# A hybrid decoder layer on one core: four experts of a block side by side, expert weights in 8 KB runs, spread products four in a row

## The chip, the core and the metric

The kernel runs on one NeuronCore of one Trainium2 chip. TensorE (PE) multiplies, VectorE (DVE), ScalarE (ACT) and GpSimd (POOL) do elementwise work, and SyncE (SP) issues nearly all loads; its own queue is called SPq in the profile. The metric is the device time of one execution in microseconds. Before the change the median of three runs is 867.6 us (866.16 to 868.55).

## The reference

One layer over 256 tokens of width 1024, all in float32. The first half (norm, input projection, a causal convolution, differential attention, output projection) is left by the change as it is. The second half is a mixture of experts:

```
h2 = rms_norm(x, norm2_g) * (1 + sc2) + sh2
scores = sigmoid(t @ w_router);  choice = scores + router_bias
# 4 of 8 groups, then 8 of 64 experts per token; gates = normed scores * 2.5
g, u = split(einsum('td,edf->tef', t, w_gu), 2)          # w_gu:   64 x 1024 x 512
routed = einsum('tef,efd->td', silu(g) * u * gate, w_down)   # w_down: 64 x 256 x 1024
x = x + g2 * (routed + shared_expert(t))
```

sc2, sh2 and g2 are slices of the conditioning product `silu(c) @ w_ada + b_ada`. All 64 experts are loaded once: 2 MiB of gate/up weights and 1 MiB of down weights each, 192 MiB in all.

## The kernel before

The kernel writes its instructions itself, in an order that a small planner in the same file sets when the program is built. Pieces of work are generators; each yields what it needs (an engine and an estimated cost, a buffer, an event), and the planner always issues the piece that can start first, by priority among near ties. What comes out is one fixed program for each engine, and each engine runs its own in order. The planner's cost of a matrix step is 0.87 whether it holds one, two or four products.

**Experts.** The routing (about 310 to 340 us) sorts the experts by the number of their tokens and puts them into 28 blocks of 128 rows ("slots"). A block is one of four kinds: H (one expert of 128 rows), M (two, with 96 and 32 rows; the 96 are multiplied as three 32-column tiles), P (two of 64) and Q (four of 32). The order is three P blocks, then PAT, `QPQQPQPPPMPHPMMMHPMPMPQPP` (line 35). I count blocks from 0: the early Q blocks are 3, 5, 6 and 8, and the late one is 25.

A block goes through these steps:
- `gather` (line 1507): a comparison on DVE makes a selection matrix, PE multiplies the split tokens with it (line 1532), for two blocks at once, and ACT applies scale and shift (line 1499) into `xt`.
- `experts` (line 1771): the gate/up product, line 1785. For each of K = 8 slices of the 1024 features, one product per tile; tiles of one block write to different rows of one bank, so they use different columns of the array. In a Q block, `parts` (line 338) cuts the four experts into two pairs, and the eight slices run first for one pair, then for the other.
- `gate_up` (line 1600): silu on ACT, product with the gate on DVE, two transpositions on PE (line 1613), a copy on ACT (line 1617).
- `tail` (line 1656): the down product, line 1676, for f in 2 slices and h in 2 halves of the output, again pair by pair in a Q block. Then per half h: times g2 on DVE (line 1688), a split into two reduced-precision halves (lines 1745 and 1747), and the products that spread the block's 128 rows over the tokens (line 1699), two for each of the 2 token tiles t, each tile into a bank of its own; DVE adds the bank to x (line 1703).
- The last block is cut finer (`finale`, `spread`) to shorten its end.

**Loads.** Weights go in pieces of 1 MiB into slots of 8 KB per partition. In the expert stage 14 slots are in turn; `advance` (line 366) gives the next piece of a fixed list to a slot as soon as the planner has the slot's last reader, and `load` (line 389) issues it on SP, behind a wait for that reader. A gate/up matrix is two pieces (halves of the 1024 rows), a down matrix one. Line 409 maps row k * 128 + p to partition p, so in a gate/up piece each partition gets four rows of 2 KB that lie 256 KB apart in memory, and in a down piece two rows of 4 KB. The first pieces of w_ada (kind "b", 256 columns) have rows of 1 KB.

**Columns.** The scale and shift of the second norm (`a2c`, `b2c`), one number per feature, must lie along partitions in the same order as the features in `h2T` and `xt`: feature k * 128 + p at partition p, column k. `ada` (line 736) makes them from the conditioning product's chunks 6 to 9: a copy to SBUF, four transpositions (line 762), and small sums on DVE.

Of the kernel before, what the change touches and what calls it, by code (L numbers as in the profile page):

```python
# [199 lines left out]
def tile_hybrid_block(ctx, tc, x, c, positions, w_ada, b_ada, norm1_g, w_in, conv_dw, conv_dw_b,  # L200
# [91 lines left out]
    params += [(rbias, bcast(router_bias, NE)), (wr, w_router[0].rearrange("(k p) n -> p k n", p=P))]  # L292
# [45 lines left out]
    def parts(kd):  # L338
        ts = tiles_of[kd]
        return [ts[0:2], ts[2:4]] if kd == "Q" else [ts]  # L340

    for b, (kd, js) in enumerate(blocks):
        gs = []
        for ts in parts(kd):
            es = sorted({t[0] for t in ts})
            gs += [("g", js[e], q) for q in range(2) for e in es]
        ds = [("d", j, 0) for j in js]
        if b == len(blocks) - 1:
            ds = [("d", j, 0, cs) for cs in ENDS for j in js]
            gs = [("g", j, q, c_) for q in range(2) for c_ in range(2) for j in js]  # L350
        order += gs + ds
# [37 lines left out]
    def load(kind, i, q, cut, now):  # L389
# [19 lines left out]
        wsrc = wsrc.rearrange("(k p) n -> p k n", p=P)  # L409
# [107 lines left out]
    pcol = cst.tile([P, 96], F32, name="pcol")  # L517
    ss = cst.tile([P, 8], F32, name="ss")
# [15 lines left out]
    nc.gpsimd.dma_start(rawb[33:49], b_ada[0, 3 * D:5 * D].rearrange("(k p) -> k p", p=P))  # L534
    nc.scalar.dma_start(rawb[49:57], vec(norm2_g, P))
# [94 lines left out]
    def late_columns():  # L630
# [3 lines left out]
        nc.tensor.transpose(p[:, 0:57], rawb[0:57], ident[0:57, 0:57])  # L634
        yield AP(57)
        nc.scalar.copy(pcol[:, 32:89], p[:, 0:57])
# [92 lines left out]
    p2 = cst.tile([P, 2, K], F32, name="p2")  # L729
# [6 lines left out]
    def ada(i, pool):  # L736
# [22 lines left out]
        else:  # L759
            yield "P", 0.43  # L760
            for j in range(4):
                nc.tensor.transpose(p[:, j * P:(j + 1) * P], s[:, j * P:(j + 1) * P], ident)
            yield pl.ev("cols")
            j = 4 * (i - 6)
            o = p2.rearrange("p a k -> p (a k)")[:, j:j + 4]
            yield TS(4)
            nc.vector.tensor_reduce(o, p.rearrange("p (j g r) -> p j g r", j=4, g=4)[:, :, :, 0], axis=AX.X, op=OP.add)
            yield TS(4)
            nc.vector.tensor_tensor(o, o, pcol[:, 65 + j:69 + j], op=OP.add)
            jj = slice(j % 8, j % 8 + 4)  # L770
            yield TS(4)
            if i < 8:
                nc.vector.tensor_copy(b2c[:, jj], p2[:, 0, jj])
            else:
                nc.vector.scalar_tensor_tensor(a2c[:, jj], p2[:, 1, jj], 1.0, pcol[:, 81:89][:, jj], op0=OP.add,
                                               op1=OP.mult)
# [462 lines left out]
    def turn(t, q):  # L1239
        d = slice(q * 512, (q + 1) * 512)  # L1240
        e = yield [TS(512), AS(512)]
        if e == "A":
            nc.scalar.activation(xn2[:, t, d], x_sb[:, t, d], AF.Copy, scale=rs2[:, t, 3:4])
        else:
            nc.vector.tensor_scalar(xn2[:, t, d], x_sb[:, t, d], rs2[:, t, 3:4], None, op0=OP.mult)
# [354 lines left out]
    def gate_up(pg, gate, put=None):  # L1600
# [11 lines left out]
        for f in range(2):  # L1612
            nc.tensor.transpose(pg[:, f * P:(f + 1) * P], act[:, f * P:(f + 1) * P], ident)
# [42 lines left out]
    def tail(b, pg):  # L1656
# [10 lines left out]
        for ts in parts(kd):  # L1667
            es = sorted({t[0] for t in ts})
            for e in es:
                yield pl.ev("L", "d", js[e], 0)  # L1670
                yield max(loaded["d", js[e]].at)
            for f in range(2):
                for h in range(2):
                    yield "P", 0.87
                    for e, o, m in ts:
                        nc.tensor.matmul(pd[h][o:o + m], aT[:, f, o:o + m],  # L1676
                                         loaded["d", js[e]].k[f][:, h * 512:(h + 1) * 512],
# [263 lines left out]
```

## Time and profile before

| what | us |
|---|---|
| median of 3 runs | 867.6 (866.16 to 868.55) |
| the profiled execution | 866.95 |
| its span, first to last instruction | 865.2 |
| PE busy | 809.2 |
| DVE busy | 464.9 |
| ACT busy | 311.2 |
| bytes read | 269.11 MB, 312 GB/s over the span |

The profile is one execution. Its page gives busy times of each engine, then 40 equal slices (21.6 us each) with the busy share in tenths, the clock that TensorE was granted (PEclk), the share of the 16 DMA engines and GB/s. "PE" counts products as they were issued; a pipelined product overlaps the next, so the step from one start to the next tells more than a single duration. A float32 product shows as two records. Views by window give, for a stretch, its length, the busy time of each engine with counts, the granted clock, the DMA share and GB/s. A row of the timeline gives start, duration, engine, line, operation, tile written <- tiles read, partitions x elements, and the number of records merged.

### The profile page before, as it was taken

To read this page: it belongs to the slowest core of one execution; us is meant where nothing else is said; L and a number is where in the kernel's file an instruction comes from. 1 tells how busy PE (TensorE), PEld (TensorE's weight loads), DVE (VectorE), ACT (ScalarE), POOL (GpSimd) and SP (SyncE) were. 2 spreads that over 40 slices of the span, in tenths; PEclk is the share of its full clock that TensorE was granted. 3 is DMA by queue.
4 is the path that set the end of the run, shared out by engine and by line. 5 is a ranking of instruction groups with operands and counts; after the bars stand their busy time and mean duration, and the time that the engine had idled before them with its cause. 6 is when DMAs were issued, how large, how long until landed. Compare 5 with 4: busy or idle time off the path is not lost.

```text
span 865.2 us, 13140 instructions
## 1 busy us (share of the span) xinstructions
PE 809.2 (94%) x4731; PEld 455.6 (53%) x4731; DVE 464.9 (54%) x1083; ACT 311.2 (36%) x682; POOL 191.6 (22%) x242
## 2 busy tenths in 40 slices
PE   3999999999858999999999999999999999999997
PEld 2897766798738776535342433434344343444233
DVE  6559999999975874206242343253433534433333
ACT  4457758667656542203020321212122121232010
POOL 3004899887514740001000000000000000000000
PEclk9999999999967999999999999999999999999999
DMA  9998678558446554999999999999999999979981
GB/s 322 366 340 288 209 253 299 184 207 273 162 152 240 187 197 176 354 389 393 355 394 397 392 397 393 392 397 393 394 392 395 374 341 362 355 278 388 398 303 50
DMA packets 127339, 271.03 MB, mean 313 GB/s; under 512 B 7085, under 2 KB 16901, under 8 KB 127272
## 3 DMA queue, kind: packets, MB, share of 16 engines
q1 hardware_dynamic: 126936, 270.00, 85.2%
q8 instruction: 37, 0.61, 0.3%
q14 instruction: 30, 0.25, 0.1%
q0 software_dynamic: 272, 0.16, 0.1%
q10 hardware_dynamic: 64, 0.02, 0.0%
HBM read 269.11 MB, written 1.05 MB: 312 GB/s over the span
## 4 chain that ended last, share of the span: by engine, by line


## 5 line engine op out<-in xcount | busy, mean ns | idle before, releaser
L1785 PE MATMUL bank<-fa 128*32 128x512 f32 (+2 forms) x1048 | 228.0, 596 | 0.1
L1703 DVE TENSOR_TENSOR fa<-fa,bank 128x512 f32<-128x512 f32 x108 | 73.3, 685 | 108.7 <-PE bank L1699 108.7
L1785 PEld LDWEIGHTS bank<-fa 128*32 128x32 f32 (+2 forms) x1048 | 63.5, 122 | 123.6 <-issue 119.2
L873 DVE SCALAR_TENSOR_TENSOR bank<-fa,tap,bank 128x256 f32<-128x256 f32 x232 | 112.9, 486 | 5.6
L1676 PE MATMUL bank<-fa 128*32 128x512 f32 (+2 forms) x496 | 111.5, 602 | 4.3 <-ACT fa L1617 4.2
L1745 ACT CAST obs<-fa 128x512 fp32r<-128x512 f32 x54 | 33.3, 619 | 150.6 <-DVE fa L1688 139.3
L1699 PE MATMUL bank<-obs,ra 128*128 128x512 f32 x216 | 78.1, 450 | 1.8 <-ACT obs L1745 0.6
L786 POOL TENSOR_TENSOR rb<-fa,rb 128x512 fp32r<-128x512 f32 x44 | 58.6, 1338 | 71.1 <-ACT rb L805 66.9
L1499 ACT ACTIVATE fa<-bank,b2c,a2c 128x256 f32<-128x256 f32 x108 | 53.2, 562 | 44.2 <-PE bank L1532 44.1
L786 POOL TENSOR_TENSOR ra<-fa,ra 128x512 fp32r<-128x512 f32 x48 | 63.9, 1339 | 21.2 <-ACT ra L805 20.6
L1699 PEld LDWEIGHTS bank<-obs,ra 128*128 128x128 f32 x216 | 33.5, 188 | 61.5 <-issue 49.7
L1532 PEld LDWEIGHTS bank<-ra 128*128 128x128 f32 x448 | 55.3, 191 | 12.3 <-issue 4.6
L1603 ACT ACTIVATE h<-bank 128x256 f32<-128x256 f32 x30 | 11.5, 383 | 135.1 <-PE bank L1785 131.1
L1532 PE MATMUL bank<-ra 128*128 128x256 f32 x448 | 59.7, 288 | 0.2 <-ACT fa L1499 0.2
L1785 PE MATMUL bank<-late_w,fa 128*64 128x512 f32 (+1 forms) x168 | 58.1, 596 | 0.0
L805 ACT CAST ra<-fa 128x512 fp32r<-128x512 f32 x76 | 46.7, 623 | 28.7 <-PE bank L822 16.3
L1609 DVE SCALAR_TENSOR_TENSOR fa<-bank,gsc,h 128x256 f32<-128x256 f32 x28 | 13.4, 482 | 75.2 <-ACT h L1603 75.2
L805 ACT CAST rb<-fa 128x512 fp32r<-128x512 f32 x68 | 42.3, 627 | 31.4 <-PE bank L822 21.8
L1676 PEld LDWEIGHTS bank<-fa 128*32 128x32 f32 (+2 forms) x496 | 26.1, 122 | 50.9 <-issue 39.7
L821 PE MATMUL bank<-ra 128*128 128x256 f32 x160 | 48.5, 303 | 3.3 <-ACT ra L1162 1.8
L1688 DVE TENSOR_TENSOR fa<-bank,fa 128x512 f32<-128x512 f32 x54 | 37.0, 686 | 25.5 <-PE bank L1676 25.5
L822 PE MATMUL bank<-ra 128*128 128x256 f32 x160 | 47.1, 295 | 0.9 <-DVE ra L1164 0.8
(380 smaller groups left out, 1375.4 us busy)
## 6 DMA issues: line engine op xcount, KB each, us to landing
fa<-in_w_exp_gu_dram SPq DMA_DIRECT2D x100, 1024.0 KB, 12.5
fa<-in_w_exp_down_dram SPq DMA_DIRECT2D x50, 1024.0 KB, 12.8
fa<-in_w_ada_dram SPq DMA_DIRECT2D x24, 1024.0 KB, 8.0
fa<-in_w_in_dram SPq DMA_DIRECT2D x22, 1024.0 KB, 7.2
late_w<-in_w_exp_gu_dram SPq DMA_DIRECT2D x19, 1024.0 KB, 14.3
late_w<-in_w_exp_down_dram SPq DMA_DIRECT2D x10, 1024.0 KB, 9.8
fa<-in_w_exp_gu_dram SPq DMA_DIRECT2D x18, 512.0 KB, 10.0
fa<-in_w_in_dram SPq DMA_DIRECT2D x12, 512.0 KB, 8.7
```

The costliest lines, as they stand in the source:

```text
L786: (nc.gpsimd if e == "G" else nc.vector).tensor_tensor(hl[:, 1], w.k[k], hl[:, 0].bitcast(F32), op=OP.subtract)
L805: nc.scalar.copy(hl[:, 0], w.k[k])
L821: nc.tensor.matmul(o, hl[:, 0, mm], src_t[:, k, 0], start=(k == 0 and m % 2 == 0), stop=False)
L822: nc.tensor.matmul(o, hl[:, 0, mm], src_t[:, k, 1], start=False, stop=False)
L873: nc.vector.scalar_tensor_tensor(cv[:, m] if j == TAPS - 1 else acc, u_sb[:, m, j:j + T], tap[:, m, j:j + 1], acc, op0=OP.mult, op1=OP.add)
L1499: nc.scalar.activation(xt[:, k, 0:ns], p3[:, f2, 0:ns], AF.Identity, bias=b2c[:, k:k + 1], scale=a2c[:, k:k + 1])
L1532: nc.tensor.matmul(p3[:, f2, 0:ns], xr[:, a, t, (f + f2) * P:(f + f2 + 1) * P], pm_[:, t, 0:ns], start=(f2 + t + a == 0), stop=(f2 + t + a ...
L1676: nc.tensor.matmul(pd[h][o:o + m], aT[:, f, o:o + m], loaded["d", js[e]].k[f][:, h * 512:(h + 1) * 512], start=(f == 0), stop=(f == 1))
L1688: nc.vector.tensor_tensor(o32, pd[h], g2b[:, h * 512:(h + 1) * 512], op=OP.mult)
L1699: nc.tensor.matmul(p, info.pT[:, t * P:(t + 1) * P], obs[h][a], start=(a == 0), stop=(a == 1))
L1703: nc.vector.tensor_tensor(x_sb[:, t, d], x_sb[:, t, d], p, op=OP.add)
L1785: nc.tensor.matmul(pg[o:o + m], info.xt[:, k, o:o + m], loaded["g", js[e]].k[k], start=(k == 0), stop=(k == K - 1))
```

## The change

Three things, and what follows from them.

1. **Runs of 8 KB.** Expert and shared-expert weights are loaded with row p * k + j (k rows a partition) instead of k * 128 + p: four neighbouring rows of gate/up, or two of down, are one run of 8 KB. The features then stand as p * 8 + k on partitions, so everything multiplied with these weights follows: the router's weights, the columns `a2c` and `b2c` (chunks 6 to 9 are now summed with eight products of one column each, into the half of the partitions that they belong to, and the bias and norm columns are loaded with 32-byte runs on POOL's queue, two loads in place of one there and one on ACT's), the tokens (the norm's result is written with a stride of 8 in its source), and `act`, whose transposition reads every second column.
2. **Four experts of a Q block side by side.** `parts` is gone. Gate/up and down steps issue all tiles of a block, and the list of loads has all first halves of a block's gate/up matrices ahead of the second halves.
3. **Spread products four in a row.** For a half h, both token tiles get their banks at once, and the four products are issued together.

```diff
-    def parts(kd):
-        ts = tiles_of[kd]
-        return [ts[0:2], ts[2:4]] if kd == "Q" else [ts]
...
-        gs = []
-        for ts in parts(kd):
-            es = sorted({t[0] for t in ts})
-            gs += [("g", js[e], q) for q in range(2) for e in es]
+        gs = [("g", j, q) for q in range(2) for j in js]
...
-        wsrc = wsrc.rearrange("(k p) n -> p k n", p=P)
+        wsrc = wsrc.rearrange("(p k) n -> p k n" if kind in ("g", "d", "sg", "sd") else "(k p) n -> p k n", p=P)
...
-    nc.gpsimd.dma_start(rawb[33:49], b_ada[0, 3 * D:5 * D].rearrange("(k p) -> k p", p=P))
-    nc.scalar.dma_start(rawb[49:57], vec(norm2_g, P))
+    nc.gpsimd.dma_start(c2[:, 0:2], b_ada[0, 3 * D:5 * D].rearrange("(a p k) -> p a k", a=2, k=K))
+    nc.gpsimd.dma_start(c2[:, 2], norm2_g[0].rearrange("(p k) -> p k", k=K))
...
-            yield "P", 0.43
-            for j in range(4):
-                nc.tensor.transpose(p[:, j * P:(j + 1) * P], s[:, j * P:(j + 1) * P], ident)
+            h = slice(64 * (i % 2), 64 * (i % 2) + 64)
+            sv = s.rearrange("p (c k) -> p k c", k=K)
+            yield "P", 1.0
+            for k in range(K):
+                nc.tensor.matmul(p[h, k:k + 1], sv[:, k], sel4[:, 0:1], start=True, stop=True)
...
+        o = xn2[:, t, d].rearrange("p (k c) -> p k c", k=4)
+        xk = x_sb[:, t].rearrange("p (c k) -> p k c", k=K)[:, 4 * q:4 * q + 4]
         if e == "A":
-            nc.scalar.activation(xn2[:, t, d], x_sb[:, t, d], AF.Copy, scale=rs2[:, t, 3:4])
+            nc.scalar.activation(o, xk, AF.Copy, scale=rs2[:, t, 3:4])
...
-            nc.tensor.transpose(pg[:, f * P:(f + 1) * P], act[:, f * P:(f + 1) * P], ident)
+            nc.tensor.transpose(pg[:, f * P:(f + 1) * P], act.rearrange("s (c f) -> s f c", f=2)[:, f], ident)
...
+        for j in js:
+            yield pl.ev("L", "d", j, 0)
+            yield max(loaded["d", j].at)
+        for f in range(2):
+            for h in range(2):
+                yield "P", 0.87
+                for e, o, m in tiles_of[kd]:
...
-            for t in range(2):
-                p = yield Get("bank")
-                yield MM(2 * 512)
+            both = yield Get("bank", 2)
+            yield MM(4 * 512)
+            for t, p in enumerate(both):
                 for a in range(2):
                     nc.tensor.matmul(p, info.pT[:, t * P:(t + 1) * P], obs[h][a], start=(a == 0), stop=(a == 1))
...
+            for k in range(K):
+                yield pl.ev("xt", b - b % 2, k // 2)
+                for j in js:
+                    yield pl.ev("L", "g", j, k // 2)
+                    yield loaded["g", j].at[k]
+                yield "P", 0.87
+                for e, o, m in tiles_of[kd]:
```

The planner sees other pieces, so the order changes in many places. Three matter below. First TensorE in block 8, a Q block: its second pair's gate/up product before (line 1785; 1699 is a spread product, 1613 the transposition of act), four slices to a row of eight.

```order
L1785 MATMUL bank_78<-fa 32x512 x8
L1699 MATMUL bank_75<-obs,ra 128x512 x2
L1699 MATMUL bank_74<-obs,ra 128x512 x2
L1785 MATMUL bank_78<-fa 32x512 x8
L1699 MATMUL bank_76<-obs,ra 128x512 x2
L1613 MATMUL bank_78<-ident,fa 128x128 x2
```

And the same block now, with all four experts (1773 is the gate/up product, 1689 the spread product, 1570 and 1573 small products that give the gates and the slots):

```order
L1773 MATMUL bank_74<-fa 32x512 x16
L1689 MATMUL bank_80<-obs,ra 128x512 x2
L1689 MATMUL bank_75<-obs,ra 128x512 x2
L1570 MATMUL bank_73<-ra 128x4 x2
L1573 LDWEIGHTS permb
L1573 MATMUL bank_73<-rtb,permb 64x256
```

Four slices hold sixteen products instead of eight, and there is one such pass in place of two. Second, TensorE in a P block of the middle part, before (1676 is the down product):

```order
L1785 MATMUL bank_80<-fa 64x512 x8
L1699 MATMUL bank_76<-obs,ra 128x512 x2
L1613 MATMUL bank_80<-ident,fa 128x128 x2
L1699 MATMUL bank_73<-obs,ra 128x512 x2
L1676 MATMUL bank_79<-fa 64x512 x2
L1699 MATMUL bank_74<-obs,ra 128x512 x2
L1676 MATMUL bank_77<-fa 64x512 x2
L1676 MATMUL bank_79<-fa 64x512 x2
L1699 MATMUL bank_76<-obs,ra 128x512 x2
```

and a P block of the same part now (1605 is the transposition, 1666 the down product, 1524 the gather):

```order
L1773 MATMUL bank_78<-fa 64x512 x8
L1689 MATMUL bank_79<-obs,ra 128x512 x2
L1689 MATMUL bank_80<-obs,ra 128x512 x2
L1773 MATMUL bank_78<-fa 64x512 x8
L1689 MATMUL bank_75<-obs,ra 128x512 x2
L1689 MATMUL bank_73<-obs,ra 128x512 x2
L1605 MATMUL bank_78<-ident,fa 128x128 x2
L1666 MATMUL bank_77<-fa 64x512 x2
L1666 MATMUL bank_79<-fa 64x512 x2
L1666 MATMUL bank_77<-fa 64x512 x2
L1524 MATMUL bank_80<-ra 128x256 x8
```

The spread products of a half stand together, and the down product directly follows the transposition. Third, SP at one place of the list of loads (the two rows between are the fetch of an expert's number), before and now:

```order
L269 DMA fa<-in_w_exp_down_dram 128x2x1024
L398 TENSOR_LOAD ids
L398 ISA x2
L269 ISA
L269 DMA fa<-in_w_exp_gu_dram 128x4x512
```

```order
L269 DMA fa<-in_w_exp_down_dram 128x2048
L391 TENSOR_LOAD ids
L391 ISA x2
L269 ISA
L269 DMA fa<-in_w_exp_gu_dram 128x2048
```

Each piece is now one run of 2048 numbers, 8 KB, for each of 128 partitions; the number of pieces is the same.

More of the change, by code (lines that the diff above doesn't have):

```diff
@@ L633, in late_columns @@
         yield "P", 0.1
-        nc.tensor.transpose(p[:, 0:57], rawb[0:57], ident[0:57, 0:57])
-        yield AP(57)
-        nc.scalar.copy(pcol[:, 32:89], p[:, 0:57])
+        nc.tensor.transpose(p[:, 0:33], rawb[0:33], ident[0:33, 0:33])
+        yield AP(33)
+        nc.scalar.copy(pcol[:, 32:65], p[:, 0:33])
         yield "P", 0.3
@@ L1666, in tail @@
         pd = yield Get("bank", 2)
[L1667 to L1677, printed above, removed]
-                                         start=(f == 0), stop=(f == 1))
-            for e in es:
-                done(("d", js[e]), 0)
+        for j in js:
[5 more added lines that the diff above has]
+                for e, o, m in tiles_of[kd]:
+                    nc.tensor.matmul(pd[h][o:o + m], aT[:, f, o:o + m],
+                                     loaded["d", js[e]].k[f][:, h * 512:(h + 1) * 512],
+                                     start=(f == 0), stop=(f == 1))
+        for j in js:
+            done(("d", j), 0)
         pl.put("aT", aT)
@@ L1694, in tail @@
             d = slice(h * 512, (h + 1) * 512)
-            for t in range(2):
-                p = yield Get("bank")
-                yield MM(2 * 512)
+            both = yield Get("bank", 2)
+            yield MM(4 * 512)
+            for t, p in enumerate(both):
                 for a in range(2):
                     nc.tensor.matmul(p, info.pT[:, t * P:(t + 1) * P], obs[h][a], start=(a == 0), stop=(a == 1))
-                if t:
-                    pl.put("ob", obs[h])
+            pl.put("ob", obs[h])
+            for t, p in enumerate(both):
                 yield TT(512)
@@ L1775, in experts @@
             pg = yield Get("bank")
[L1776 to L1793 removed]
+            for k in range(K):
+                yield pl.ev("xt", b - b % 2, k // 2)
+                for j in js:
+                    yield pl.ev("L", "g", j, k // 2)
+                    yield loaded["g", j].at[k]
+                yield "P", 0.87
+                for e, o, m in tiles_of[kd]:
+                    nc.tensor.matmul(pg[o:o + m], info.xt[:, k, o:o + m], loaded["g", js[e]].k[k],
+                                     start=(k == 0), stop=(k == K - 1))
+                if b < 2 and k % 4 == 1:
+                    for j in js:
+                        if loaded["g", j].off[k // 4] != LAST:
+                            advance(pl.cur.ready, loaded["g", j].off[k // 4])
+                if k % 4 == 3:
+                    for j in js:
+                        done(("g", j), k // 4)
             info.users[0] -= 1
@@ L1905, in tile_hybrid_block @@
                 for f in range(2):
-                    nc.tensor.transpose(B[2 + t][:, f * P:(f + 1) * P], act[:, f * P:(f + 1) * P], ident)
+                    nc.tensor.transpose(B[2 + t][:, f * P:(f + 1) * P], act.rearrange("s (c f) -> s f c", f=2)[:, f],
+                                        ident)
                 nc.scalar.copy(aT.rearrange("p f s -> p (f s)"), B[2 + t][:, 0:T])
```

43 lines of the change are left out of this document (10 added, 33 removed).

## The prediction

> **What bounds the kernel now.** I read the page first, its busy times and its 40 slices.
>
> ```profile
> PE 809.2 (94%) x4731; PEld 455.6 (53%) x4731; DVE 464.9 (54%) x1083; ACT 311.2 (36%) x682; POOL 191.6 (22%) x242
> PE   3999999999858999999999999999999999999997
> DMA  9998678558446554999999999999999999979981
> GB/s 322 366 340 288 209 253 299 184 207 273 162 152 240 187 197 176 354 389 393 355 394 397 392 397 393 392 397 393 394 392 395 374 341 362 355 278 388 398 303 50
> ```
>
> From slice 16 on (346 us) TensorE and the DMA engines are both at 9: two resources run level through the expert stage, so taking time from one alone would soon meet the other. Next, starts of blocks on TensorE in order of time (line 1785 is the gate/up product). Blocks are counted from 0: P P P, then the 25 letters of PAT. Block 9 is the first P after the early Q blocks, 25 is the late Q, 26 and 27 the last two P.
>
> ```profile
> 538.92 0.64 PE L1785 MATMUL bank<-late_w,fa 128*64 128x512 f32 x1
> 804.30 0.62 PE L1785 MATMUL bank<-fa 128*32 128x512 f32 x2
> 828.50 0.65 PE L1785 MATMUL bank<-fa 128*64 128x512 f32 x2
> ```
>
> The windows between them (and one just ahead of the routed loads, when nothing was being moved):
>
> ```profile
> 328.00:331.80 3.80, 3.80 (x27) 3.35 (x26) 2.76 (x22) 0.00 (x0) 0.00 (x0) 1.00 0.00 0
> 331.80:538.90 207.10, 203.80 (x1025) 85.18 (x1023) 69.21 (x169) 42.30 (x88) 5.55 (x4) 1.00 0.99 371
> 538.90:804.30 265.40, 258.21 (x1496) 109.63 (x1495) 104.69 (x230) 61.72 (x127) 0.00 (x0) 1.00 1.00 372
> 804.30:865.20 60.90, 53.65 (x247) 18.76 (x246) 22.28 (x40) 5.88 (x12) 0.00 (x0) 0.99 0.65 240
> ```
>
> The second number is the window's length, then TensorE's busy time; the last two are DMA share and GB/s. I call the three stages A (blocks 2 to 8, four of them Q), B (blocks 9 to 24, no Q) and C (25 to the end). TensorE works 203.8 of 207.1 us in A and 258.2 of 265.4 in B. Nobody is far behind it: in A the DMA moved 371 x 207.1 = 76.8 MB, while block 9's first half needs blocks 2 to 8 and 2 MiB more, 68 MiB = 71.3 MB. So the DMA was some 5.5 MB, 14 us, ahead of TensorE when block 9 began.
>
> **The rate of a load goes by its run.** Three short windows in which one kind of load fills the queue, with issues of SP that lie ahead of them, and the page's time from issue to landing:
>
> ```profile
> fa<-in_w_exp_gu_dram SPq DMA_DIRECT2D x100, 1024.0 KB, 12.5
> fa<-in_w_exp_down_dram SPq DMA_DIRECT2D x50, 1024.0 KB, 12.8
> fa<-in_w_ada_dram SPq DMA_DIRECT2D x24, 1024.0 KB, 8.0
> ...
> 19.30 4.59 SPq L269 DMA_DIRECT2D fa<-in_w_ada_dram  x2
> 28.00:30.00 2.00, 2.00 (x19) 2.00 (x18) 1.63 (x6) 0.97 (x2) 0.00 (x0) 1.00 1.07 350
> 433.10 4.96 SPq L269 DMA_DIRECT2D fa<-in_w_exp_gu_dram  x3
> 442.00:444.00 2.00, 2.00 (x10) 0.70 (x6) 0.88 (x3) 0.00 (x0) 0.00 (x0) 1.00 1.05 387
> 498.68 6.92 SPq L269 DMA_DIRECT2D fa<-in_w_exp_down_dram  x3
> 514.00:516.00 2.00, 2.00 (x18) 1.75 (x18) 0.00 (x0) 2.00 (x5) 0.00 (x0) 1.00 1.03 410
> ```
>
> Runs of 1 KB move at 350 GB/s, of 2 KB (gate/up) at 387, of 4 KB (down) at 410, each with the share at its ceiling. Per engine (a sixteenth) a run takes 46.8, 84.7 and 159.8 ns: 37.7 ns for each KB and about 9 ns besides. An 8 KB run would then take 310.7 ns, 422 GB/s. That is an extrapolation; its bounds are 410 (no better than the longest run seen) and 434 (no fixed part left, 1 KB in 37.7 ns). I take 421, since a few last loads stay at 2 and 4 KB. The present mix of two gate/up MiB to one down MiB is 3 / (2/387 + 1/410) = 394.
>
> The Trainium skill, "DMA: Bandwidth & Descriptors", section "Why small descriptors are slow (HBM only)", prices a packet at a fixed 3 cycles beside one cycle per 32 bytes. By that 2 KB costs 67 cycles per 64 and 8 KB 259 per 256, a gain of 3.5%, where the rows above already show 10.6% from 1 to 2 KB and 5.9% from 2 to 4. By it the mix would rise from 394 to about 405, and the sum below would come out 7 us longer.
>
> **Four experts side by side.** In a Q block one k step is now two steps, one per pair. What a step costs with two and with four products on it stands in the trace, since the M blocks already issue four (three 32-column tiles of one expert, one of another):
>
> ```profile
> 515.74 3.63 PE L1785 MATMUL bank<-fa 128*32 128x512 f32 x16
> 519.29 0.98 PE L1532 MATMUL bank<-ra 128*128 128x256 f32 x6
> 589.00 3.64 PE L1785 MATMUL bank<-fa 128*32 128x512 f32 x32
> 592.57 0.38 PE L1578 MATMUL bank<-ra 128*128 128x2 f32 x2
> ```
>
> A float32 product shows as two records. Half a Q pair (4 steps, 16 records) takes 3.55 us to the next group, half an M block (4 steps, twice the records) 3.57: four cost what two do, 0.86 us a step without the change-over. A Q block so loses 8 gate/up steps and 4 down steps, 12 x 0.86 = 10.3 us of TensorE: 41 us for four blocks in A, none in B, 10.3 in C. The price: a step waits for the last of four loads, and on TensorE's queue the spread products of the block before and the gathers of the next stand behind it, for which VectorE and ScalarE wait. In A, where loads set the pace, those engines have nothing else that is late; in B there is no Q, and block 25's loads are there when it starts. SP's loads keep their number; in a Q block the four first halves now come ahead of the four second ones, so slots come free in fours, and with 14 slots ten others are still out when the first four are used, 25 us of loads.
>
> **The products of spread.** They switch the array from narrow tiles to full width and back.
>
> ```profile
> 566.19 1.08 PE L1676 MATMUL bank<-fa 128*64 128x512 f32 x4
> 567.20 0.74 PE L1699 MATMUL bank<-obs,ra 128*128 128x512 f32 x2
> 567.86 1.94 PE L1676 MATMUL bank<-fa 128*64 128x512 f32 x8
> 575.53 1.20 PE L1699 MATMUL bank<-obs,ra 128*128 128x512 f32 x4
> 576.66 0.64 PE L1785 MATMUL bank<-late_w,fa 128*64 128x512 f32 x1
> PE bank L1676 <- ACT fa L1617: 4.2, 9, 0.5
> PE bank L1613 <- DVE fa L1609: 3.0, 8, 0.4
> ```
>
> A pair takes 0.66 us to the next group, four in a row 1.13, so two products cost 0.47 and the change-over back 0.19. The step ahead of a pair takes 1.01 us instead of 0.86, the change-over there 0.15. One visit fewer saves 0.34. Counted in the order, B goes from 63 visits to 47 (16 x 0.34 = 5.4 us) and, with the block boundaries shifted, holds ten spread products more (2.3 us). The waits in B sum to 7 us (last two rows: the down product for its operand, the transposition for its gate). Four spread products ahead of a transposition cover most of the second, 3.0 us; three more transpositions than before go straight to their own down products, at up to 0.5 each. B gains 5.4 - 2.3 + 3.0 - 1.5, about 5 us. Bounds: nothing (two banks at once come late) and 9.
>
> **The rest of the change.** The strided columns: the four transpositions of an "ada" chunk become eight products with one column each. Rows nearest:
>
> ```profile
> L762 PE MATMUL bank<-ident,fa 128*128 128x128 f32 x16 | 2.5, 276 | 0.8 <-ACT fa L748 0.8
> L1138 PE MATMUL bank<-ones,fa x4: 212/352/352, 257.9 to 258.4; 128*128 128x1 f32 x4
> 100.00:225.00 125.00, 119.24 (x786) 95.86 (x784) 120.96 (x260) 91.83 (x240) 104.20 (x145) 1.00 0.67 231
> 225.00:250.00 25.00, 17.57 (x106) 12.02 (x106) 22.02 (x53) 12.56 (x32) 9.57 (x9) 0.86 0.60 211
> 250.00:275.00 25.00, 16.86 (x89) 14.88 (x90) 14.73 (x38) 16.38 (x36) 8.71 (x11) 0.59 0.48 168
> L1245 DVE TENSOR_SCALAR fa<-fa,rs x2: 468/477/486, 313.7 to 322.7; 128x512 f32<-128x512 f32 x2
> ```
>
> Four chunks cost 2.5 us now; one-column records start some 0.17 us apart at 257.9 (four in 0.5 us, at a low clock), 0.09 at the full one, so 16 records take 1.4 to 2.7 us a chunk, 3 to 8 us more in all. They lie between 100 and 225 us, where VectorE works 121 of 125 us on the convolution and sets the end, and TensorE then idles 15 us from 225 to 275. I cost them at 0; without that cover, 3 to 8. VectorE loses three or four 0.2 to 0.7 us operations a chunk and gains two, about 0. The strided read of the second norm (line 1245, 0.48 us) sits on the path to the routing: 0 to +0.5, I take 0, as I do for the strided act of a transposition (at worst its time doubles, 0.2 us in 19 blocks, 4 us). POOL issues two strided loads in place of one, when it is idle until 30 us; the router's weights come early either way.
>
> **The sum**, against the profiled execution (span 865.2, time 866.95).
> - A: without the 14 us of lead, the DMA brought 71.3 MB in 193 us; at 394 GB/s they take 181, so 12 us were holes (slots held by the first blocks). At 421: 169 + 12 = 181 us. TensorE's own work falls to 203.8 - 41 = 163, so the DMA now sets A's end: block 9 starts at 331.8 + 181 + 1 = 514, 25 us earlier.
> - B: starts with no lead, block 9's other loads come 5 and 10 us after the first: +2.5. After that a P or M block costs TensorE 16.3 us (265.4 / 16 = 16.6 less 0.3) and the DMA 6.3 MB / 421 = 14.9, so TensorE sets the pace: 265.4 - 5 + 2.5 = 263. Block 25 starts at 777.
> - C: Q took 24.2 us (804.30 to 828.50), now 13.9; the last 36.7 stay: 50.6, end at 827.6. Its loads: when block 25 starts, the 14 slots of 1 MiB hold its own 12 MiB and two of block 26; the other ten MiB follow from the first freed slot on (3.5 us later) in 25 us, so the last lands 30 us after 777, at 807, while block 27 starts at 805 and needs its down weights some 9 us later.
> Span 828, with the 1.75 us around it 829.5. The median lies 0.65 above the profiled time: **830 us**.
>
> **Rivals.**
> 1. Longer runs buy less. For: 8 KB is not in the trace. At 410, A ends 5 us later: 835. At 394, 12 us later: 842. The rule cited above gives 837 this way.
> 2. The clock. With slack in A, TensorE waits between bursts of 3.5 us for 4 MiB that take 10 us. The two windows at 225 and 250 above show what happens when it works 17 of 25 us: 0.86 and 0.59 granted. Against: A's work is 163 of 181 us. From a mean clock under 163/181 = 0.90 TensorE sets A again; at 0.8 A takes 204, block 9 starts at 537, and with 260 for B and 50.6 for C the time is 850. The Trainium skill, "TensorE: Matmul & The Clock Gate", Part 1, states the mechanism: an idle window of about 3.4 us halves the clock, and it comes back after a busy one. By that, bursts begin slow and the loss stays within the slack.
> 3. The four do not overlap as M's do (four different weights, some in late_w): Q costs as before. A and C then stay and B alone gains its 5: 538.9 + 260 + 60.9 + 2.4 = 862.
> 4. The other side: loads get slower. Partitions of a gate/up load now read 16 KB apart, where the present ones read neighbouring 2 KB; no load of the trace does so. After 331.8 the DMA moves 190 MB less the 1 MB output; with 12 us of holes and the 27 us that now follow the last load, the end passes 865 when 189 / r exceeds 494 us, r under 383 GB/s. At 370 it is 331.8 + 12 + 511 + 27 + 2 = 884. Where those 27 us are from:
>
> ```profile
> 838.00:842.00 4.00, 4.00 (x20) 1.55 (x22) 1.48 (x3) 0.37 (x1) 0.00 (x0) 1.00 0.30 96
> 842.00:846.00 4.00, 4.00 (x21) 1.21 (x16) 2.30 (x4) 1.23 (x2) 0.00 (x0) 1.00 0.01 4
> ```
>
> At the rate of a full queue 96 GB/s over 4 us is 1 us of loads: the last one lands at about 839, some 27 us ahead of the end.
> 5. The change does nothing net (re-planned order loses what it wins): 867.
>
> **How the numbers follow.** The forecast's case, 816 to 842, gets 0.66; rival 1 at full size 0.08; rival 2 0.12; rival 3 0.06; rival 4 0.06; rival 5 0.02. The range of 8 in 10 is 814 to 853: it leaves out rivals 3 to 5 and a few per cent at either end. Faster by over 0.3% (what a measurement of this kernel can tell from none) takes all but 4 and 5: 0.92; same 0.02; slower 0.06.
>
> **What would show it.** Right: windows of 8 KB loads at about 421 GB/s; block 9 at about 514, block 25 at 777; a Q block's 32-record half in 3.6 us; TensorE idle in A with waits for DMA, and none in B. Wrong: gate/up windows still at 387 or under; PEclk under 9 through A; half a Q block taking 7 us; or block 9 as late as 535 with the DMA ahead of it again.

## The result

The changed kernel takes 833.49 us (median of 4 runs, 833.11 to 834.26), the kernel before 867.88 beside it (866.16 to 868.55): a ratio of 0.9608, 95% interval 0.9591 to 0.9624. The profiled run took 833.57 us with a span of 831.7. On other chips, where the experiments ran, the kernel before took 868.6 to 869.1.

The page of the changed kernel: busy times and three rows of the 40 slices.

```profile
PE 772.5 (93%) x4779; PEld 461.1 (55%) x4779; DVE 459.9 (55%) x1074; ACT 314.9 (38%) x685; POOL 193.7 (23%) x246
PE   3999999799987999999998897999999999999896
DMA  9998767645564684789999999999999999797992
GB/s 312 364 347 289 269 217 260 202 160 197 203 203 151 211 330 169 265 342 393 422 420 421 421 421 421 421 422 420 421 420 421 421 398 377 295 387 297 424 407 96
```

From slice 19 to 31 (counted from 0) the loads run at 420 to 422 GB/s, where full slices stood at 392 to 397. TensorE has two 8s and a 7 in slices 21 to 24, where it had 9s; the DMA has two 7s near the end, where it had one. Starts of blocks 9, 25 and 26 on TensorE, in order of time (line 1773 is now the gate/up product):

```profile
516.11 1.07 PE L1773 MATMUL bank<-fa 128*64 128x512 f32 x2
...
780.97 0.62 PE L1773 MATMUL bank<-fa 128*32 128x512 f32 x2
...
793.68 0.65 PE L1773 MATMUL bank<-fa 128*64 128x512 f32 x2
```

The three stages by windows (length, then busy us of PE, PEld, DVE, ACT and POOL with their records, granted clock, DMA share, GB/s):

```profile
331.80:516.10 184.30, 171.70 (x1023) 79.52 (x1021) 65.87 (x166) 41.52 (x86) 5.87 (x4) 1.00 0.96 389
516.10:781.00 264.90, 258.09 (x1513) 117.28 (x1513) 108.92 (x241) 63.86 (x130) 0.00 (x0) 1.00 0.96 393
781.00:831.70 50.70, 41.89 (x235) 15.65 (x234) 17.80 (x32) 4.74 (x10) 0.00 (x0) 0.97 0.72 282
```

Stage A is 22.8 us shorter (207.1 to 184.3), B 0.5 (265.4 to 264.9), C 10.2 (60.9 to 50.7): together the 33.5 us by which the span fell. In A TensorE now idles 12.6 us. The waits put 5.5 of it down to loads and 3.2 to the gate that the transposition needs, with nothing else queued ahead of it; the rest are waits for other operands from ACT and DVE. In B one short wait for a load is left:

```profile
PE bank L1605 <- DVE fa L1601: 3.2, 3, 1.1
PE bank L1666 <- DMA fa<-in_w_exp_down_dram: 2.3, 2, 1.4
PE bank L1773 <- DMA late_w<-in_w_exp_gu_dram: 1.4, 1, 1.4
PE bank L1666 <- DMA late_w<-in_w_exp_down_dram: 1.4, 1, 1.4
PE bank L1773 <- DMA fa<-in_w_exp_gu_dram: 0.4, 1, 0.4
```

```profile
PE bank L1666 <- ACT fa L1609: 5.5, 12, 0.5
PE bank L1773 <- DMA fa<-in_w_exp_gu_dram: 0.3, 1, 0.3
```

The first fence is of A, the second of B (us in total, times, longest). The last Q block of A, block 8, in the timeline of TensorE:

```profile
493.96 3.64 PE L1773 MATMUL bank<-fa 128*32 128x512 f32 x32
...
499.01 2.14 PE L1773 MATMUL bank<-fa 128*32 128x512 f32 x6
502.60 0.62 PE L1773 MATMUL bank<-late_w,fa 128*32 128x512 f32 x1 [1.45 <-DMA late_w<-in_w_exp_gu_dram]
```

A half whose loads are there takes 3.64 us, with all four experts in it. The second half begins with the products whose loads have landed and then waits for the last.

### The profile page after: what moved, and what is told of

Read it like the earlier page. It is cut to its first block, busy times and chain, and to the rows that moved or that the text cites. A ratio compares the mean times of both kernels' runs of the same rounds, so it can differ in the third digit from the quotient of the medians.

```text
span 831.7 us, 13232 instructions
## 1 busy us (share of the span) xinstructions
PE 772.5 (93%) x4779; PEld 461.1 (55%) x4779; DVE 459.9 (55%) x1074; ACT 314.9 (38%) x685; POOL 193.7 (23%) x246
## 4 chain that ended last, share of the span: by engine, by line
## 5 line engine op out<-in xcount | busy, mean ns | idle before, releaser
L1773 PE MATMUL bank<-fa 128*32 128x512 f32 (+2 forms) x1032 | 198.6, 596 | 0.7 <-DMA fa<-in_w_exp_gu_dram 0.7
L1773 PEld LDWEIGHTS bank<-fa 128*32 128x32 f32 (+2 forms) x1032 | 57.7, 123 | 108.6 <-issue 100.6
L1666 PE MATMUL bank<-fa 128*32 128x512 f32 (+2 forms) x496 | 97.9, 600 | 8.7 <-ACT fa L1609 6.5
L1693 DVE TENSOR_TENSOR fa<-fa,bank 128x512 f32<-128x512 f32 x108 | 69.5, 682 | 49.2 <-PE bank L1689 47.0
L776 POOL TENSOR_TENSOR rb<-fa,rb 128x512 fp32r<-128x512 f32 x46 | 60.6, 1325 | 64.7 <-ACT rb L795 62.9
L1689 PE MATMUL bank<-obs,ra 128*128 128x512 f32 x216 | 65.4, 423 | 2.8 <-ACT obs L1735 1.9
L1524 PE MATMUL bank<-ra 128*128 128x256 f32 x448 | 59.4, 288 | 0.4 <-ACT fa L1491 0.4
L1689 PEld LDWEIGHTS bank<-obs,ra 128*128 128x128 f32 x216 | 36.7, 188 | 39.7 <-issue 27.0
L1773 PE MATMUL bank<-late_w,fa 128*32 128x512 f32 (+1 forms) x184 | 50.8, 596 | 1.4 <-DMA late_w<-in_w_exp_gu_dram 1.4
L1666 PEld LDWEIGHTS bank<-fa 128*32 128x32 f32 (+2 forms) x496 | 24.4, 121 | 46.8 <-issue 30.9
L811 PE MATMUL bank<-ra 128*128 128x256 f32 x160 | 47.8, 299 | 1.4 <-ACT ra L577 1.4
L812 PE MATMUL bank<-ra 128*128 128x256 f32 x160 | 45.9, 287 | 0.1
```

What stands on the lines that cost most here:

```text
L776: (nc.gpsimd if e == "G" else nc.vector).tensor_tensor(hl[:, 1], w.k[k], hl[:, 0].bitcast(F32), op=OP.subtract)
L811: nc.tensor.matmul(o, hl[:, 0, mm], src_t[:, k, 0], start=(k == 0 and m % 2 == 0), stop=False)
L812: nc.tensor.matmul(o, hl[:, 0, mm], src_t[:, k, 1], start=False, stop=False)
L1524: nc.tensor.matmul(p3[:, f2, 0:ns], xr[:, a, t, (f + f2) * P:(f + f2 + 1) * P], pm_[:, t, 0:ns], start=(f2 + t + a == 0), stop=(f2 + t + a ...
L1666: nc.tensor.matmul(pd[h][o:o + m], aT[:, f, o:o + m], loaded["d", js[e]].k[f][:, h * 512:(h + 1) * 512], start=(f == 0), stop=(f == 1))
L1689: nc.tensor.matmul(p, info.pT[:, t * P:(t + 1) * P], obs[h][a], start=(a == 0), stop=(a == 1))
```

## The experiments

Times are medians. The first five take the change apart; a table of them stands behind the fifth.

One caution for all the windows below. They belong to one execution of each kernel, and they all begin at 331.8 us, where the first routed load of the kernel before is issued. In the other profiles that load is issued between 329.5 and 335.3 us, so a window that begins at 331.8 counts up to 3.5 us of the part ahead of the routed loads into stage A, or leaves up to 2.3 us of A out. The table counts from each kernel's own first routed load (SP's timeline) to its block 9. The last column is the time in which loads stood still: the length less what the bytes moved would take at the full rate of that kernel's mix (394, 397.7, 413.6 or 421 GB/s). In the last row block 9 follows three Q blocks and not four.

| kernel | first routed load | block 9 | between | loads stood still |
|---|---|---|---|---|
| before | 331.86 | 538.9 | 207.0 | 12.1 |
| changed | 332.03 | 516.1 | 184.1 | 13.6 |
| only 8 KB runs | 330.49 | 537.9 | 207.4 | 17.7 |
| only four side by side | 329.51 | 521.0 | 191.5 | 10.2 |
| only spread in fours | 330.44 | 532.3 | 201.9 | 11.8 |
| without the fours in a row | 330.56 | 515.1 | 184.5 | 12.3 |
| with pairs in the Q blocks | 335.27 | 539.7 | 204.4 | 17.0 |
| runs of 4 KB | 334.32 | 525.4 | 191.1 | 15.1 |
| runs of 2 KB | 333.87 | 526.6 | 192.7 | 12.5 |
| one Q moved | 329.56 | 500.1 | 170.5 | 14.2 |

### Only the 8 KB runs

```diff
 # the changed kernel with both of these back as they were:
+    def parts(kd):
+        ts = tiles_of[kd]
+        return [ts[0:2], ts[2:4]] if kd == "Q" else [ts]
...
-            both = yield Get("bank", 2)
-            yield MM(4 * 512)
+            for t in range(2):
+                p = yield Get("bank")
+                yield MM(2 * 512)
```

> Only the 8 KB runs are kept (with the strided columns they need): a Q block again works its experts in two pairs, and a block's spread products go out in pairs. Theory of the prediction: TensorE worked 203.8 of the 207.1 us of stage A before the change and still does, so faster loads only lengthen the DMA's lead: block 9 starts at 538 to 541, stage B stays at 265 to 267, stage C at 60 to 61, 865 to 870 us in all, with the DMA held back for free slots (fewer than 380 GB/s over A). Rival (the loads already set stage A's end before the change): block 9 at 515 to 526 and 842 to 853 us.

Measured: 870.79 us against 868.70, ratio 1.0026 (1.0011 to 1.0041). Its three stages by windows, and the two longest waits of SP's queue in stage B, for slots that the gate/up and the down products still hold:

```profile
331.80:537.90 206.10, 202.84 (x1014) 84.86 (x1012) 68.20 (x163) 41.99 (x87) 5.56 (x4) 1.00 0.96 387
537.90:803.60 265.70, 259.00 (x1495) 110.96 (x1494) 104.81 (x230) 61.60 (x127) 0.00 (x0) 1.00 0.91 364
803.60:866.70 63.10, 54.39 (x247) 19.17 (x246) 22.17 (x40) 5.90 (x12) 0.00 (x0) 0.99 0.57 218
```

```profile
SPq L269 <- PE bank L1784: 134.9, 32, 11.9
SPq L269 <- PE bank L1675: 59.3, 14, 6.7
```

The three longest in the kernel before (1699 is a spread product):

```profile
SPq L269 <- PE bank L1785: 88.2, 24, 11.8
SPq L269 <- PE bank L1676: 39.7, 11, 6.7
SPq L269 <- PE bank L1699: 24.8, 15, 4.1
```

Loads that are 7% faster end nothing sooner: block 9 starts at 537.9 against 538.9, and SP stands longer in front of slots that TensorE has not yet freed: 200.2 us over all six rows of that view, against 177.8 before. The rival, loads as the bound of A, falls. The loss of 2 us is in stage C (63.1 against 60.9), where the last spread products now stand ahead of block 26 and wait (timeline of TensorE):

```profile
828.56 0.50 PE L1698 MATMUL bank<-obs,ra 128*128 128x512 f32 x1 [0.64 <-ACT obs L1744]
829.32 0.50 PE L1698 MATMUL bank<-obs,ra 128*128 128x512 f32 x1 [0.25 <-DVE obs L1746]
```

### Only four side by side

```diff
     def parts(kd):
-        ts = tiles_of[kd]
-        return [ts[0:2], ts[2:4]] if kd == "Q" else [ts]
+        return [tiles_of[kd]]
```

> The kernel before with the four experts of a Q block side by side, and nothing else: gate/up loads keep runs of 2 KB, spread products go out in pairs. Theory of the prediction: the DMA sets stage A at the old mix of 394 GB/s: 71.3 MB take 181 us, with 12 us of holes 193, block 9 at 526; stage B 265.4 + 2.5 without a lead = 268; stage C 50.6; with the 2.4 us around it 846 to 848 us. Rival (the four do not overlap): 865 to 869. Rival (the longer runs carried nearly all of the 34 us): 858 to 866.

Measured: 848.62 us, ratio 0.9776 (0.9752 to 0.9801), a little above the 846 to 848 expected. Its windows:

```profile
331.80:521.00 189.20, 174.75 (x1008) 79.62 (x1006) 65.74 (x159) 41.22 (x85) 5.57 (x4) 0.97 1.00 376
521.00:793.10 272.10, 263.06 (x1507) 112.41 (x1506) 110.23 (x241) 63.98 (x130) 0.00 (x0) 1.00 1.03 389
793.10:844.90 51.80, 44.44 (x237) 15.46 (x236) 18.26 (x32) 4.74 (x10) 0.00 (x0) 0.96 0.69 249
```

Stage A ends 5 us earlier than the theory had it (521 against 526), of which 2.3 us is an earlier start of the routed loads; B takes 4 us more (272.1 against 268), C 1.2 more. The four overlap, and they carry most of the gain by themselves.

### Only the spread products four in a row

```diff
-            for t in range(2):
-                p = yield Get("bank")
-                yield MM(2 * 512)
+            both = yield Get("bank", 2)
+            yield MM(4 * 512)
+            for t, p in enumerate(both):
...
```

> The kernel before with the four spread products of a half block issued in a row, and nothing else. Theory of the prediction: each visit fewer saves 0.34 us of TensorE; 16 visits fewer and covered waits give 5 us in stage B, and as TensorE sets stage A too there, up to 2 us more: 859 to 863 us. Rival (what the visits win is given back in waits of the transpositions and down products, as stage B of the changed kernel, shorter by only 0.5 us, suggests): 865 to 868.

Measured: 856.91 us, ratio 0.9877 (0.9849 to 0.9905): 11.8 us, more than the theory's 6 to 10. Its stages A and B:

```profile
331.80:532.30 200.50, 197.68 (x1014) 84.40 (x1012) 65.13 (x160) 41.32 (x85) 5.08 (x4) 1.00 1.00 373
532.30:791.60 259.30, 253.76 (x1504) 112.97 (x1502) 105.77 (x236) 62.64 (x128) 0.00 (x0) 1.00 1.02 383
```

B gains 6.1 us, near the 5 of the theory; A gains 6.6 by the windows, about 5 from the first routed load on (207.0 to 201.9), where 2 were allowed. As long as TensorE sets the pace in A, a visit saved there is time saved, as in B.

### The changed kernel without the fours in a row

The previous diff turned round, on the changed kernel.

> The changed kernel with the spread products in pairs again; 8 KB runs and four side by side are kept. Theory of the prediction: stage B loses its 5 us, from 264.9 to 270, stages A and C hardly change (the DMA sets A): 837 to 840 us. Rival (the fours bring nothing net): 833 to 835 us.

Measured: 840.50 us, ratio 0.9677 (0.9653 to 0.9701), against 0.9608 with them: 0.7%, some 6 us. Its stages:

```profile
331.80:515.10 183.30, 173.39 (x1012) 81.20 (x1011) 66.08 (x160) 41.26 (x85) 5.56 (x4) 0.97 0.97 395
515.10:785.20 270.10, 261.84 (x1507) 112.80 (x1506) 110.21 (x241) 63.99 (x130) 0.00 (x0) 1.00 0.96 389
785.20:835.80 50.60, 43.06 (x237) 15.49 (x236) 18.32 (x32) 4.75 (x10) 0.00 (x0) 0.99 0.65 248
```

B is 270.1 against 264.9: 5.2 us, as the theory had it. A and C are within 1 us, so in A, where loads now set the end, the same edit that won 5 us alone wins next to nothing. Groups of stage B (busy us, mean ns of one, then idle time ahead of them), first here, then in the changed kernel:

```profile
L1689 PE MATMUL bank<-obs,ra 128*128 128x512 f32 x134 | 48.5, 451 | 1.6 <-DVE obs L1737 1.1 <-ACT obs L1735 0.5
L1605 PE MATMUL bank<-ident,fa 128*128 128x128 f32 x32 | 7.3, 308 | 3.0 <-DVE fa L1601 3.0
```

```profile
L1689 PE MATMUL bank<-obs,ra 128*128 128x512 f32 x136 | 40.9, 422 | 0.9 <-ACT obs L1735 0.6 <-DVE obs L1737 0.3
L1605 PE MATMUL bank<-ident,fa 128*128 128x128 f32 x32 | 7.4, 313 | 0.0
```

Two more spread products show 7.6 us less in the busy time of their group, and the transposition's wait of 3.0 us is covered. A group's busy time contains what overlaps its neighbours: TensorE's own falls by 3.8 us (261.84 to 258.09).

### The changed kernel with pairs in the Q blocks

```diff
-        gs = [("g", j, q) for q in range(2) for j in js]
+        gs = []
+        for ts in parts(kd):
+            es = sorted({t[0] for t in ts})
+            gs += [("g", js[e], q) for q in range(2) for e in es]
 # the gate/up and down products in two pairs likewise
```

> The changed kernel with the experts of a Q block in two pairs again; 8 KB runs and spread products four in a row are kept. If each part acts for itself: the time of the 8 KB runs alone (870.8) less what the fours in a row won alone (868.7 - 856.9 = 11.8): 859 us, block 9 at 531 to 533. If the longer runs can be used once spread is shorter: 848 to 855.

Measured: 860.81 us, ratio 0.9908 (0.9881 to 0.9934). The sum of the two parts by themselves gives 859.0, so in the time they neither help nor hinder each other much. Block 9 was expected at 531 to 533 and came at 539.7 in the profiled execution, the slowest of the four (864.48 us; the others 860.26 to 861.01). Its stages A and C:

```profile
331.80:539.70 207.90, 204.18 (x1047) 90.23 (x1045) 70.76 (x191) 42.90 (x88) 5.08 (x4) 1.00 0.94 379
...
798.40:862.60 64.20, 53.40 (x244) 19.00 (x242) 21.04 (x36) 5.99 (x12) 0.00 (x0) 0.98 0.62 245
```

Beside the spread products alone (856.9), the longer runs look 4 us slower. The two profiles are 9.9 us apart. The first routed load comes 4.8 us later here (335.27 against 330.44), A is 2.6 us longer from that load on, B 0.6 shorter and C 3.1 longer (61.1 there). The loss in C is again in block 25, as with the 8 KB runs alone: four spread products stand and wait ahead of block 26, which starts 26.1 us after block 25, against 24.2 in the kernel before. What makes A longer stays open.

| kept of the change | us | before beside it | difference |
|---|---|---|---|
| 8 KB runs | 870.79 | 868.70 | +2.1 |
| four side by side | 848.62 | 868.70 | -20.1 |
| spread in fours | 856.91 | 868.70 | -11.8 |
| runs, spread | 860.81 | 868.64 | -7.8 |
| runs, four | 840.50 | 868.70 | -28.2 |
| all three | 833.49 | 867.88 | -34.4 |

The longer runs lose 2 us alone and win 8.1 (848.6 to 840.5) once four side by side has made loads the bound of A. In the profiles 7.0 of it is in A, from the first routed load on (191.5 to 184.5), 2.0 in B and 1.2 in C.

### Shorter runs, nothing else

Each partition's 16 KB of gate/up is dealt to the two halves in pieces of 4 KB, and in the second kernel of 2 KB; the number and size of the loads stay, and the order of the eight k steps follows the pieces.

```diff
-        if kind != "b":
+        if kind == "g":
+            wsrc = wsrc.rearrange("p (a q k) n -> p q a k n", q=2, k=2)[:, q]   # k=1 for 2 KB
+        elif kind != "b":
             wsrc = wsrc[:, q * nk:(q + 1) * nk]
```

> The changed kernel with the gate/up loads in runs of 4 KB (each partition's half is two runs of 4 KB, 16 KB from a pair to the next; the order of the k steps follows), in one load of 1 MiB as before; down loads keep 8 KB. If a load's rate goes by the length of its runs alone: 410 GB/s for gate/up, a mix of 3 / (2/410 + 1/421) = 413.6, stage A 3 us longer than the changed kernel's (block 9 at 519), stage B as it is, since TensorE sets it: 836 to 838 us. If the rate comes from something else of the change (the whole weight of a partition lying together): no change, 833 to 835, or a rate under 400 and 845 or more.

> The same with gate/up in runs of 2 KB that lie 4 KB apart in a partition's 16 KB, where the kernel before read 2 KB rows that neighbour those of the next partition. If the length of a run sets the rate: 387 GB/s, a mix of 397.7, stage A 8 to 10 us longer (block 9 at 524 to 526), stage B near its balance (6.3 MB in 15.8 us a block against 16.5 of TensorE): 842 to 846 us. If rows that lie apart cost more than neighbours: below 380 GB/s in gate/up, stage B set by loads too, 855 us or more.

Measured: 837.91 us with 4 KB, ratio 0.9627 (0.9590 to 0.9665), and 843.06 with 2 KB, ratio 0.9698 (0.9669 to 0.9728). A window of steady loads of the 4 KB kernel, then of the 2 KB kernel:

```profile
425.00:450.00 25.00, 23.90 (x166) 14.36 (x163) 12.11 (x30) 8.50 (x18) 2.96 (x2) 1.00 1.02 414
```

```profile
425.00:450.00 25.00, 23.90 (x170) 14.60 (x166) 11.66 (x28) 8.94 (x19) 2.95 (x2) 1.00 1.04 400
```

From 400 to 675 us the windows of 25 us give 411 to 414 and 393 to 401 GB/s, the rates of the mixes (413.6 and 397.7), and both times lie in the ranges given. Between these layouts only the length of a run shows: rows of 2 KB that lie 4 KB apart move as fast as neighbouring ones did.

Block 9 was less well met: 525.4 with 4 KB where 519 was expected, and 526.6 with 2 KB where it was 524 to 526. From the first routed load on, A is 191.1 and 192.7 us against 184.1, so 7.0 longer where 3 were expected, and 8.6 where it was 8 to 10. Of the 4 KB kernel only the slowest execution (841.38 us) has a profile; in it the granted clock is at 0.50 from about 517 to 524 us, in the last Q block of A, which is some 3 us of work.

### One Q block moved

```diff
-PAT = "QPQQPQPPPMPHPMMMHPMPMPQPP"
+PAT = "QPQPQPPPMPHPMMQMHPMPMPQPP"
```

The changed kernel leaves two idle times, TensorE's in A and the DMA's late in B, where slots are held (windows of the changed kernel):

```profile
500.00:525.00 25.00, 19.43 (x97) 6.32 (x97) 4.51 (x9) 1.99 (x4) 0.00 (x0) 1.00 1.01 421
675.00:700.00 25.00, 24.54 (x104) 9.97 (x100) 11.19 (x25) 3.03 (x6) 0.00 (x0) 1.00 0.96 368
700.00:725.00 25.00, 24.08 (x174) 11.70 (x174) 10.17 (x23) 6.66 (x14) 0.00 (x0) 1.00 0.78 313
```

> The changed kernel with one letter of the block order moved: the third of the early Q blocks goes to the middle of the program (QPQPQPPPMPHPMMQMHPMPMPQPP); every block is the same work. Theory from the trace of the changed kernel: TensorE idles some 12 us in stage A for loads, while the loads are held up for slots later (368, 313, 392 and 321 GB/s in the four windows from 675 to 775, against 421: 3.1 + 6.4 + 1.7 + 5.9 = 17 us of loads). One Q later should take 10 to 13 us off: 820 to 824 us. Rival (TensorE's 472 us of work in the expert stage already set the end, the two idle times can't be traded): 831 to 835. Rival (a Q among M and H blocks makes a new wait of 10 us for its 12 MiB): 835 to 845.

Measured: 821.83 us, ratio 0.9465 (0.9432 to 0.9497): 12 us faster than the changed kernel by the same work in another order. Windows of it, up to block 9 and from there to block 25:

```profile
331.80:500.10 168.30, 163.36 (x959) 79.02 (x959) 64.98 (x161) 41.21 (x85) 5.87 (x4) 1.00 0.96 390
500.10:766.50 266.40, 257.96 (x1558) 117.34 (x1555) 108.26 (x240) 64.03 (x130) 0.00 (x0) 1.00 1.00 413
```

TensorE's idle time up to block 9 falls from 12.6 to 4.9 us, and the middle moves 413 GB/s against 393 in about the same time, with a Q block in it. The two idle times could be traded, but that is only half of the gain. From the first routed load to the end the changed kernel takes 499.7 us and this one 487.9; TensorE's idle time falls by 5.8 us (28.2 to 22.4), and its busy time by 6.0 (471.5 to 465.5) with the same 2763 records. The fall in busy time is in the gate/up products (208.0 to 204.4) and the down products (106.1 to 103.4). That fits what block 8 shows: where the loads come late, the products of a step no longer run side by side.

### All Q blocks spread

```diff
-PAT = "QPQQPQPPPMPHPMMMHPMPMPQPP"
+PAT = "HPMQPPMPQPPMPQMHPMQPPMPQP"
```

> The changed kernel with all five Q blocks spread evenly over the order (HPMQPPMPQPPMPQMHPMQPPMPQP), every block the same work. Same theory, further: the loads are never held and TensorE waits hardly anywhere; TensorE's 472 us of the expert stage, some 7 us of operand waits and the last 9 us give 812 to 819 us. Rivals: no gain over one Q moved (820 to 824), as the loads of the last Q then come late (5 to 10 us at its start); or none at all (831 to 835).

Measured: 831.97 us, ratio 0.9574 (0.9546 to 0.9602). The theory missed by 13 to 20 us; the time is that of the rival by which nothing is gained. Windows of it:

```profile
375.00:400.00 25.00, 24.58 (x115) 13.49 (x113) 5.90 (x21) 5.47 (x12) 0.00 (x0) 1.00 0.73 294
400.00:425.00 25.00, 24.44 (x141) 9.90 (x138) 7.84 (x24) 3.12 (x8) 1.27 (x1) 1.00 0.92 378
425.00:450.00 25.00, 25.00 (x153) 12.98 (x152) 14.13 (x32) 7.42 (x16) 2.56 (x2) 1.00 0.70 268
775.00:800.00 25.00, 18.47 (x97) 5.41 (x96) 6.67 (x12) 2.36 (x5) 0.00 (x0) 0.98 1.01 420
```

From 375 to 450 TensorE is fully busy with other work (the shared expert among it), so slots come free late: 7.5 + 2.6 + 9.1 = 19 us of loads are lost (each the window's shortfall from 421). At the other end the last Q waits for its loads, and behind that the granted clock is at half from about 798.5 to 806, which is up to 3.4 us of work. The next order keeps two Q blocks at the front, which need loads where TensorE has other work, and moves the last Q forward.

```diff
-PAT = "QPQQPQPPPMPHPMMMHPMPMPQPP"
+PAT = "QPQPPPQPMPHPMQMMHPMPQPMPP"
```

> The changed kernel with the block order QPQPPPQPMPHPMQMMHPMPQPMPP: two Q blocks stay at the front, the other three are spread, the last of them two blocks ahead of where it was. It tests why the even spread gained nothing: there the loads stood at 294, 378 and 268 GB/s from 375 to 450 us, held for slots by products that wait behind TensorE's other work of that time, and the last Q waited for loads. If that is the reason, two Q blocks at the front avoid the first and an earlier last Q the second: 817 to 823 us, as with one Q moved. If Q blocks late in the order cost by themselves: 828 to 835.

Measured: 819.69 us, ratio 0.9438 (0.9413 to 0.9463), in the range of the theory, the fastest of all and level with one Q moved (821.83, 819.25 to 823.53). Which of the two repairs mattered how much was not separated.

## Why the prediction was right

The mechanism was right: loads at a higher rate set the end of A once four side by side had taken TensorE's work there, TensorE sets B, and the time (830 against 833.49) and every stage came out near. Some terms were mis-sized, and B and C were met with some luck, by errors that cancel.

**The rate of loads.** 421 GB/s was an extrapolation, and 420 to 422 is what stands there; the kernels with 4 and 2 KB put 411 to 414 and 393 to 401 under it. Rival 1 falls. The Trainium skill, "DMA: Bandwidth & Descriptors", section "Why small descriptors are slow (HBM only)", with its fixed 3 cycles a packet, gives an estimate of 3.5% from 2 to 8 KB; from 387 to 421 it is 8.8%, so the trace decides against it.

**Four side by side.** A half Q block with its loads there takes 3.64 us (3.6 foretold), and block 25 to 26 12.71 (13.9). Rival 3 falls. In A TensorE's busy time fell by 32, not 41; one cause is in the timeline of block 8, where a step starts with the loads that have landed and its products no longer run side by side. Where TensorE waits for the next load anyway, as in block 8, that costs nothing; the kernel with one Q moved gets 6 us of it back.

**Stage A.** Block 9 at 516.1 against 514. The sum had 169 us of loads and 12 us of holes, time in which loads stand still because slots are held. From the first routed load on, A is 184.1 us, and 390 GB/s leave (421 - 390) / 421 x 184.1 = 13.6 us of holes, so the term was near; the table ahead of the experiments has it at 10.2 to 15.1 us in the kernels whose A is bound by loads (those with four side by side). It is not quite fixed, though. In the kernels with spread products in pairs, the step from 394 to 421 gave A 7.0 us (191.5 to 184.5) and not the 12 of the sum, with 2.1 us more of holes and 1.1 MB (2.6 us) more loaded ahead of block 9. Between the changed kernel and the one with 2 KB runs, where little else than the gate/up runs differs, the step from 397.7 to 421 gave 8.6 (192.7 to 184.1), near the 9.9 that 71.3 MB come to. What moves the holes by 2 to 3 us was not separated; the planner's order is not the same in these kernels.

**Stage B.** 264.9 against 263, and here a sum was met by luck. Without the fours B takes 270.1, which is 4.7 more than before, against 2.5 + 2.3 = 4.8 for the start without a lead and the shifted boundaries. But no product of B waits for a load in that kernel, so the 2.5 is not there; in the changed kernel the first half of block 9 loses 1.4 us to late loads. What stands in the place of the 2.5 is 1.1 us more of idle time, in waits of the spread products, and TensorE's work: it grows by 3.6 us (258.2 to 261.8), of which seven more spread products (127 to 134) account for 2.4, where the sum had 2.3. The fours win 5.2 (6.1 by themselves) against 5.4 + 3.0 - 1.5 = 6.9. The wait of 3.0 is gone, and the down product's wait is 5.5, against 4.2 before and 3.7 without the fours, near the 1.5. What was costed at nothing and wasn't is the transposition of a strided operand: 313 ns a record against 290 in the kernel with the fours alone (row below, its stage B); with the products in pairs it is 308 against 288. Over 32 records that is 0.7 us.

```profile
L1613 PE MATMUL bank<-ident,fa 128*128 128x128 f32 x32 | 6.7, 290 | 0.0
```

**Stage C and the early part.** C took 50.7 against 50.6, with block 25 1.2 us shorter and the rest 1.3 longer, two errors that cancel. The last load lands at about 814 us and not at 807, still in time: no product of C waits for a load. The first gate/up product starts at 337.15; before, at 336.98. So between these two executions the 64 one-column products and the strided reads ahead of the routing cost 0.2 us together. Other executions spread wider: that product starts at 334.6 to 337.0 in the three profiles of kernels without the strided columns, and at 334.7 to 340.4 in the nine with them. That the cover held is likely, but a cost of up to a few us is not excluded.

**The clock, rival 2.** In the changed kernel's profile the clock stays at 1.00 in A, though TensorE worked only 19.43 of 25 us from 500 on. In the kernel without the fours it does fall there (2 us windows):

```profile
504.00:506.00 2.00, 1.28 (x6) 0.46 (x6) 0.20 (x1) 0.37 (x1) 0.00 (x0) 1.00 1.00 418
506.00:508.00 2.00, 1.17 (x4) 0.18 (x2) 0.00 (x0) 0.00 (x0) 0.00 (x0) 0.70 1.02 426
508.00:510.00 2.00, 1.43 (x6) 0.20 (x8) 0.00 (x0) 0.00 (x0) 0.00 (x0) 0.50 1.01 422
510.00:512.00 2.00, 2.00 (x12) 0.39 (x8) 0.00 (x0) 0.00 (x0) 0.00 (x0) 0.50 1.01 422
```

With the next two (0.59) that is about 7 us at half the clock, some 3 us of work lost, and the same kernel has a shorter drop from 444 to 449. Windows of 2 us show such drops after the routing in four of the twelve kernels profiled: this one, four side by side alone (three drops), the 4 KB runs and all Q blocks spread. So the rival was real in kind and far smaller than it was priced: over A the granted clock is 0.97 at its lowest, where the 20 us stood on 0.8. Its page, the Trainium skill's "TensorE: Matmul & The Clock Gate", Part 1, has half the clock after an idle window of 3.4 us; the half agrees, while the fall here followed a stretch that was still some 60% busy.

**Rivals 4 and 5** are refuted by the result; the strided reads of rival 4 by the 2 KB kernel as well.

## What to carry to other kernels

Where two resources run nearly level, relieving the one that does not set the end is worth nothing by itself: the longer runs lost 2 us alone and won 8 once TensorE, which four side by side alone relieved by 20 us, was out of the way. Price an edit in the stage where its resource sets the end. Before stages of two executions are compared, count each from its own first event: here the start differed by up to 5.8 us. When each resource then idles in another stage, the order of the work is the next thing to change: here 12 to 14 us for a few letters.

## What the runs showed of the hardware

- Loads from HBM went at 420 to 422 GB/s in runs of 8 KB, and mixes of two thirds 4 KB or 2 KB (the rest 8 KB) at 411 to 414 and 393 to 401. The 2 KB pieces lay 4 KB apart; the mix of neighbouring 2 KB rows and 4 KB runs in the kernel before went at 391 to 396.
- The granted clock fell to 0.50 for some 3 to 7 us after the routing in four of the twelve kernels profiled. In the kernel without the fours the longer drop followed about 5 us in which TensorE was busy some 60% of the time; in the changed kernel 6 us at 47% (506 to 512 us) were followed by none. The busy share alone does not tell here when the clock falls.
- Ahead of the routing, the mean granted clock from 100 to 300 us is 0.91 in the three profiles whose first gate/up product starts at 339.0 to 340.4 us (pairs in the Q blocks, 4 KB, 2 KB) and 0.93 to 0.95 in the nine where it starts at 334.6 to 338.1. So a part of the spread between executions goes with the clock there. Over whole runs the picture is mixed: with 4 KB runs the four go from 833.71 us at a mean clock of 0.986 to 841.38 at 0.975, while the changed kernel took 833.11 at 0.976 and 833.57 at 0.984.
- A transposition that reads every second element of its operand took 313 ns a record against 290, and 308 against 288 in the kernels with spread products in pairs.
